# A decoder layer on one core: the first input projection issued between the first transposes, its weights moved up, the low-rank weights moved back

## The chip, the cores and the metric

The kernel runs on one core of a Trainium2 chip. The metric is the device time of one execution in microseconds (us); lower is better. Five engines work side by side, each from its own queue and in the order of that queue: TensorE (PE; its weight loads are PEld), VectorE (DVE), ScalarE (ACT), GpSimd (POOL) and SyncE (SP), which here issues the DMAs.

## The reference

One layer of a decoder trunk on 1024 tokens of width 1024, in float32. The part at the beginning of the kernel is the norm of the tokens and the mixer's input projection:

```python
h = _rms_norm(x, norm_pre_mix[i])
...
p = h @ w_in.astype(h.dtype)
u = p[..., :GLU_COLS]
q = p[..., GLU_COLS:]
q = q + (_token_shift(q) - q) * mu.astype(h.dtype)
...
r, k, v = q[..., :o1], q[..., o1:o2], q[..., o2:o3]
wd, ad, gd = q[..., o3:o4], q[..., o4:o5], q[..., o5:o6]
wf = (decay_w0 + jnp.tanh(wd) @ decay_up).astype(jnp.float32)
...
a = jax.nn.sigmoid(iclr_a0 + ad @ iclr_up)
g = jax.nn.sigmoid(gd) @ gate_up
```

Behind it come a recurrence over the tokens (eight heads of 64), a causal convolution of width 31 on a gated part of the projection, the output projection, a second norm, and a feed-forward part with a convolution of width 3 and 2816 channels. Both parts add their normed results to x.

## The kernel before

The tokens are worked on in two halves of 512 (`h` is 0 or 1). Channels lie on the 128 partitions, so the rows of x (128 tokens each) are normed and then transposed on TensorE. Every float32 operand of a projection is split in two, a rounded `hi` (or `wh` for weights) and the rest `lo` (`wl`), and three matmuls are added: wh x hi, wh x lo, wl x hi.

**The beginning.** `setup` loads an identity matrix (`const`, first 128 columns), all parameters (`params`) and the other constants; `setup_mixer` allocates, loads the low-rank weights (`lora`, and two pieces through the ring `wr` into `lw`, split by an ACT cast, line 232, and a POOL subtraction, line 234), and scales parameters on DVE (lines 238 to 247). `mixer` loads four rows of x (lines 281 to 285, eight DMAs of 256 KB), and then for each pair of rows, which is 256 tokens, runs `norm_rows` and `channels`. `norm_rows` takes the mean square of the first row of a pair on ACT (line 302) and that of the second on DVE (`bn_stats`, line 295), raises to the power -0.5 on POOL (line 153) and scales each row, its first half on ACT (line 305) and its second on DVE (line 306). `channels` transposes (line 146) into four PSUM banks of two channel blocks each (tags `pe` and `pb`), and evicts each block with the norm's weight: `hi` on ACT (line 271), `lo` on DVE (line 273). Both need `params`.

**The projections.** `project` multiplies one block of 128 output columns (64 for `w`, the low-rank inputs of decay and rate). Its weights come in two pieces of 256 KB, one for channel blocks 0 to 3 and one for 4 to 7. `weight` loads a piece into `wr` (a ring of three buffers), casts it to `wh` on ACT and subtracts on POOL to `wl` (line 158; `wh` and `wl` have two buffers each, so a cast waits until PE has done with the piece two before). For the first token half, `wl` is also stored to DRAM (`lows`, line 179), and the second token half loads it from there. The very first projection (`halves`, block 0 of `k0`) is done in two groups of 24 matmuls over 256 tokens each; all others are 24 matmuls over 512. The order of the first ones is k0 (two blocks), w, k1 (two), r0 (two), r1 (two). Then the elementwise work of the first quarter of the tokens begins.

**What sets the order.** The kernel is written for a planner, which orders each engine's instructions in a modelled timeline: of what is ready, it takes that with the lowest number first. A number is normally the place in the program; a `stream` gives its block numbers that begin elsewhere (first -1000, rwkv 1000, norm 200000, conv 300000, proj 400000), and `high_priority`, which `weight` and `shift` use, sets it to 0. On the chip, each engine then follows its planned order. `issue_after` puts instructions of an engine behind a named one of the same engine.

Of the kernel before, what the change touches and what calls it, by code (L numbers as in the profile page):

```python
# [21 lines left out]
P = 128  # L22
# [72 lines left out]
class Trunk:  # L95
# [87 lines left out]
    def setup(self):  # L183
# [13 lines left out]
        nc.sync.dma_start(self.params, a["params"])  # L197
        nc.sync.dma_start(self.const[:, P:], a["consts"][:, P:])
# [10 lines left out]
    def setup_mixer(self, ctx):  # L209
# [13 lines left out]
        self.Y = self.psum.tile([P, 512], F32, name="Y")  # L223


        self.lora = cp.tile([G_LORA, D_RWKV], F32, name="lora")
        nc.sync.dma_start(self.lora, a["lora"][:G_LORA, 2])
        self.lw = cp.tile([96, 2, D_RWKV], F32R, name="lw")
# [6 lines left out]
        self.lx = cp.tile([96, 2, QUARTER], F32R, name="lx")  # L235
        n = POFF["k_k"]
        self.omu = cp.tile([P, n], F32, name="omu")
        nc.vector.tensor_scalar(self.omu, self.params[:, :n], -1.0, 1.0, ALU.mult, ALU.add)

        self.hw0 = cp.tile([P, 8], F32, name="hw0")  # L240
        nc.vector.tensor_scalar(self.hw0, self.params[:, POFF["w0"]:POFF["w0"] + 8], 0.5, None, ALU.mult)
        self.ka = cp.tile([P, 8], F32, name="ka")
# [5 lines left out]
        self.carry = cp.tile([P, n], F32, name="carry")  # L248
        self.ccarry = cp.tile([P, 4, CONV_W - 1], F32, name="ccarry")
# [31 lines left out]
    def load_rows(self, h, rows):  # L281
        for t, row in enumerate(rows):
            rs = slice(h * HALF + t * P, h * HALF + (t + 1) * P)
            for j in range(2):
                self.nc.sync.dma_start(row[j], self.a["x"][rs, j * 512:(j + 1) * 512])

    def norm_rows(self, rows):

        nc = self.nc
        for t, row in enumerate(rows):  # L290
            ss = self.small.tile([P, 4], F32, tag="ss", name=self.nm("ss"))
            if t % 2:
                bs = self.small.tile([P, 4, 6], F32, tag="gn", bufs=3, name=self.nm("bs"))[:, 0:2]
                for j in range(2):
                    nc.vector.bn_stats(bs[:, j], row[j])
# [10 lines left out]
            nc.vector.tensor_scalar(row[1], row[1], ss[:, 3:4], None, ALU.mult)  # L306


    def project(self, src, m, hs, halves=False, kept=None):


        ps = self.bank()
        low = lambda j: kept and (kept[0], self.lows[kept[1], j])
        if halves:
            ws = [self.weight(src[j], [P, 4, m], kept=low(j)) for j in range(2)]
            for ts in (slice(0, 256), slice(256, 512)):
                for k in range(KT):
                    (wh, wl), (hi, lo) = ws[k // 4], hs[k]
                    self.mm(ps[:m, ts], wh[:, k % 4], hi[:, ts], start=k == 0, stop=False)
                    self.mm(ps[:m, ts], wh[:, k % 4], lo[:, ts], start=False, stop=False)  # L320
                    self.mm(ps[:m, ts], wl[:, k % 4], hi[:, ts], start=False, stop=k == KT - 1)
            return ps
# [759 lines left out]
    def mixer(self, sts):  # L1082
# [85 lines left out]
        with self.stream("norm"):  # L1168
            two = [self.tl("l8", [P, 2, D]) for _ in range(2)]
            rows = [cut(two[t // 2][:, t % 2]) for t in range(4)]  # L1170
            with self.stream("first"):
                self.load_rows(0, rows)
# [7 lines left out]
        project(0, hs, "k0 w k1 r0 r1")  # L1180
# [129 lines left out]
```

## Time and profile before

| what | us |
|---|---|
| median of three runs | 1310.73 |
| lowest and highest | 1307.76, 1311.3 |
| the profiled execution | 1310.48 |
| its span in the profile | 1308.7 |

The profile shows one execution. Its times count from the start of the span, and the 1.8 us between the execution's time and its span lie around it. A group "x4" in a timeline row is four instructions in a row; the two numbers at its beginning are its start and its length, and the brackets at its end say how long the engine had been idle and for what it had waited. Matmuls overlap one another, so the distance of their starts says more of their rate than their durations.

### The profile page before, as it was taken

To read this page: it belongs to the slowest core of one execution; us is meant where nothing else is said; L and a number is where in the kernel's file an instruction comes from. 1 tells how busy PE (TensorE), PEld (TensorE's weight loads), DVE (VectorE), ACT (ScalarE), POOL (GpSimd) and SP (SyncE) were. 2 spreads that over 40 slices of the span, in tenths; PEclk is the share of its full clock that TensorE was granted. 3 is DMA by queue.
4 is the path that set the end of the run, shared out by engine and by line. 5 is a ranking of instruction groups with operands and counts; after the bars stand their busy time and mean duration, and the time that the engine had idled before them with its cause. 6 is when DMAs were issued, how large, how long until landed. Compare 5 with 4: busy or idle time off the path is not lost.

```text
span 1308.7 us, 22940 instructions
## 1 busy us (share of the span) xinstructions
PE 1260.4 (96%) x8580; PEld 1018.6 (78%) x8580; DVE 864.0 (66%) x1520; ACT 678.4 (52%) x1354; POOL 462.6 (35%) x412
## 2 busy tenths in 40 slices
PE   5999989999999989999999999999999999999996
PEld 4767767777779867878799788888888888888884
DVE  5276997996789989995521364355455438479567
ACT  6563663656855765657642464443433445444451
POOL 4343320111123322444462466676766540000001
PEclk9999989999999989999999999999999999999998
DMA  6554332243333351222354765666564433335326
GB/s 236 160 146 125 115 112 90 83 145 113 115 110 106 119 181 43 73 66 78 100 161 126 265 211 167 194 183 195 173 207 137 120 92 113 94 110 164 105 65 209
DMA packets 97167, 176.77 MB, mean 135 GB/s; under 512 B 10560, under 2 KB 17088, under 8 KB 97056
## 3 DMA queue, kind: packets, MB, share of 16 engines
q1 hardware_dynamic: 97056, 175.31, 43.5%
q8 instruction: 67, 1.10, 0.4%
q14 instruction: 44, 0.36, 0.1%
HBM read 139.62 MB, written 35.65 MB: 134 GB/s over the span
## 4 chain that ended last, share of the span: by engine, by line
PE 77%; DVE 14%; ACT 4%; DMA 2%; issue 2%; POOL 1%; SPq 0%; POOLq 0%; ACTq 0%; DVEq 0%
PE pb L131 63%; PE pe L131 5%; DVE pc L410 4%; PE pn L131 3%; PE xs L131 3%; DVE dw L587 1%; PE pe L146 1%; DMA x<-x1d 1%; DVE pt L479 1%; DVE nrow L971 1%; DMA pt<-mixd 1%; DVE kk L480 1%; POOL wl L158 1%; PE pc L146 0%; DVE m L158 0%
## 5 line engine op out<-in xcount | busy, mean ns | idle before, releaser
L131 PE MATMUL pb<-f,wh 128*128 128x512 f32 x1408 | 444.5, 396 | 3.6 <-ACT pb L782 1.8
L158 POOL TENSOR_TENSOR wl<-wr,wh 128x512 fp32r<-128x512 f32 (+1 forms) x240 | 316.3, 1319 | 360.9 <-ACT wh L158 332.4
L158 ACT CAST wh<-wr 128x512 fp32r<-128x512 f32 (+1 forms) x279 | 171.5, 615 | 296.0 <-PE pb L131 142.3
L131 PEld LDWEIGHTS pb<-f,wh 128*128 128x128 f32 x1408 | 265.1, 189 | 63.9 <-ACT pb L782 2.0
L131 PE MATMUL pb<-f,wl 128*128 128x512 f32 x704 | 280.6, 399 | 1.7 <-POOL wl L158 1.5
L131 PE MATMUL pb<-h,wh 128*128 128x512 f32 (+3 forms) x720 | 230.0, 399 | 1.9 <-ACT wh L158 1.0
L888 DVE SCALAR_TENSOR_TENSOR acc<-pb,params,acc 128x511 f32<-128x511 f32 (+1 forms) x128 | 95.4, 745 | 184.8 <-ACT acc L883 124.0
L410 DVE SCALAR_TENSOR_TENSOR pc<-c,params,pc 128x512 f32<-128x512 f32 x232 | 174.1, 751 | 8.3 <-ACT pc L407 4.4
L131 PEld LDWEIGHTS pb<-f,wl 128*128 128x128 f32 x704 | 133.1, 189 | 34.6 <-POOL wl L158 3.9
L131 PEld LDWEIGHTS pb<-h,wh 128*128 128x128 f32 (+2 forms) x720 | 132.0, 189 | 34.4 <-ACT wh L158 2.7
L131 PE MATMUL pb<-h,wl 128*128 128x512 f32 (+3 forms) x360 | 146.3, 406 | 2.7 <-POOL wl L158 2.5
L153 POOL TENSOR_TENSOR ss<-var,mhalf 128x1 f32<-128x1 f32 x16 | 11.0, 693 | 229.7 <-DVE ss L952 203.3
L131 PE MATMUL pb<-w,a 128*128 128x512 f32 x366 | 89.8, 393 | 0.0
L131 PEld LDWEIGHTS pb<-h,wl 128*128 128x128 f32 (+2 forms) x360 | 67.8, 188 | 21.8 <-POOL wl L158 5.1
L131 PE MATMUL pb<-wh,a 128*128 128x512 f32 x240 | 81.5, 396 | 0.0
L131 PEld LDWEIGHTS pb<-w,a 128*128 128x128 f32 x366 | 68.7, 188 | 16.1
L928 POOL TENSOR_TENSOR b<-b,b 128x512 f32<-128x512 f32 x44 | 57.0, 1295 | 0.9
L888 DVE SCALAR_TENSOR_TENSOR pt<-pb,params,pt 128x511 f32<-128x511 f32 (+1 forms) x48 | 35.7, 744 | 31.5 <-ACT ecarry L885 31.0
L131 PEld LDWEIGHTS pb<-wh,a 128*128 128x128 f32 x240 | 45.1, 188 | 10.6
L700 POOL TENSOR_TENSOR XG<-r,GE 64x256 f32<-64x256 f32 x30 | 20.8, 696 | 85.5 <-DVE r L719 80.8
L883 ACT ACTIVATE acc<-pb,params 128x512 f32<-128x512 f32 x64 | 49.5, 773 | 1.8 <-PE pb L131 1.8
L131 PE MATMUL pb<-wl,a 128*128 128x512 f32 x120 | 47.7, 397 | 0.0
(301 smaller groups left out, 2038.8 us busy)
## 6 DMA issues: line engine op xcount, KB each, us to landing
wr<-ffn_up SPq DMA_DIRECT2D x176, 256.0 KB, 2.7
wr<-w_in SPq DMA_DIRECT2D x80, 256.0 KB, 2.9
b<-ffn_down SPq DMA_DIRECT2D x44, 256.0 KB, 3.9
sums<-b SPq DMA_DIRECT2D x44, 256.0 KB, 2.4
wr<-sums SPq DMA_DIRECT2D x44, 256.0 KB, 2.7
lows<-wl SPq DMA_DIRECT2D x40, 256.0 KB, 3.2
wl<-lows SPq DMA_DIRECT2D x40, 256.0 KB, 2.6
wr<-ffn_down SPq DMA_DIRECT2D x33, 256.0 KB, 2.7
```

Source lines behind the costliest of these rows:

```text
L131: return self.nc.tensor.matmul(out, lhsT, rhs, start=start, stop=stop, skip_group_check=skip)
L146: self.nc.tensor.transpose(out, in_, self.con("ident")[:n, :n])
L158: return self.nc.scalar.copy(hi, src), eng.tensor_tensor(lo, src, hi.bitcast(F32), ALU.subtract)
L410: nc.vector.scalar_tensor_tensor(out, c[:, j:j + HALF], w(j), acc, ALU.mult, ALU.add)
L479: nc.vector.tensor_tensor_scan(sg[:, l], self.con("scan"), sg[:, l], 0.0, ALU.mult, ALU.add)
L480: nc.vector.scalar_tensor_tensor(kk[:, l], k[:, l], self.par("k_k", 2 * pp + l), kk[:, l], ALU.mult, ALU.mult)
L587: nc.vector.tensor_tensor(dv[:, j + 1:, :j], dv[:, j + 1:, :j], tv, ALU.add)
L700: nc.gpsimd.tensor_tensor(x[64:128], R[64:128, gs], w.GE[64:128, c, gs].unsqueeze(2).broadcast_to([64, 4, CH]), ALU.mult)
L883: nc.scalar.activation(acc, ps, AF.Identity, scale=w(2), bias=self.par("fb", ch))
L888: nc.vector.scalar_tensor_tensor(acc[:, o:], ps[:, :HALF - o], w(j), acc[:, o:], ALU.mult, ALU.add)
L928: sub = lambda o, x, y, op=ALU.subtract: nc.gpsimd.tensor_tensor(o, x, y, op)
L971: nc.vector.tensor_tensor(out, a, b, op)
```

## The change

The loads of `params` and of the other constants are taken from `setup`. In `mixer`, inside the stream "first", the loads of the first two rows are followed by the two pieces of the first projection's weights (`self.first`, by `weight`, with its cast, its subtraction and its store), the load of `params`, the loads of the other two rows, and the other constants. `project` takes those weights for its first block, and its result is accumulated in the bank `pc` instead of `pb`. The low-rank loads, casts and subtractions become `low_rank`, called behind the projections k0 and w; the parameter scalings become `scales`, called ahead of k0. In `norm_rows`, the second `bn_stats` of an odd row is put behind the scaling of the row before it on DVE.

```diff
@@ -194,8 +194,6 @@
         self.const = cp.tile([P, NCONST], F32, name="const")
         with self.stream("first"):
             nc.sync.dma_start(self.const[:, :P], a["consts"][:, :P])
-        nc.sync.dma_start(self.params, a["params"])
-        nc.sync.dma_start(self.const[:, P:], a["consts"][:, P:])
         self.mhalf = cp.tile([P, 8], F32, name="mhalf")
         nc.gpsimd.memset(self.mhalf, -0.5)
         self.mixd = self.dp.tile([SEQ, D], F32, name="mixd")
@@ -221,32 +219,40 @@
         self.dw = cp.tile([P, 16 + 1024], F32, name="dw")
         nc.gpsimd.memset(self.dw[0:64, 528:1040], 0.0)
         self.Y = self.psum.tile([P, 512], F32, name="Y")
-
-
         self.lora = cp.tile([G_LORA, D_RWKV], F32, name="lora")
+        self.lw = cp.tile([96, 2, D_RWKV], F32R, name="lw")
+        self.lx = cp.tile([96, 2, QUARTER], F32R, name="lx")
+        n = POFF["k_k"]
+        self.omu = cp.tile([P, n], F32, name="omu")
+        self.hw0 = cp.tile([P, 8], F32, name="hw0")
+        self.ka = cp.tile([P, 8], F32, name="ka")
+        self.carry = cp.tile([P, n], F32, name="carry")
+        self.ccarry = cp.tile([P, 4, CONV_W - 1], F32, name="ccarry")
+
+    def low_rank(self):
+
+
+        nc, a = self.nc, self.a
         nc.sync.dma_start(self.lora, a["lora"][:G_LORA, 2])
-        self.lw = cp.tile([96, 2, D_RWKV], F32R, name="lw")
         for e in range(2):
             raw = self.wp.tile([P, D_RWKV], F32, tag="wr", bufs=3, name=self.nm("wr"))
             nc.sync.dma_start(raw, a["lora"][:, e])
             nc.scalar.copy(self.lw[:, e], raw[0:96])
             low = self.lw[64:96, e]
             nc.gpsimd.tensor_tensor(low, raw[64:96], low.bitcast(F32), ALU.subtract)
-        self.lx = cp.tile([96, 2, QUARTER], F32R, name="lx")
+
+    def scales(self):
+
+        nc = self.nc
         n = POFF["k_k"]
-        self.omu = cp.tile([P, n], F32, name="omu")
         nc.vector.tensor_scalar(self.omu, self.params[:, :n], -1.0, 1.0, ALU.mult, ALU.add)
 
-        self.hw0 = cp.tile([P, 8], F32, name="hw0")
         nc.vector.tensor_scalar(self.hw0, self.params[:, POFF["w0"]:POFF["w0"] + 8], 0.5, None, ALU.mult)
-        self.ka = cp.tile([P, 8], F32, name="ka")
         ka = self.params[:, POFF["k_a"]:POFF["k_a"] + 4]
         nc.vector.tensor_scalar(self.ka[:, 0:4], ka, 0.5, None, ALU.mult)
         nc.vector.tensor_scalar(self.ka[:, 4:8], ka, -0.5, 1.0, ALU.mult, ALU.add)
         cw = self.params[:, POFF["cw"]:POFF["cw"] + 4 * CONV_W]
         nc.vector.tensor_scalar(cw, cw, 0.5, None, ALU.mult)
-        self.carry = cp.tile([P, n], F32, name="carry")
-        self.ccarry = cp.tile([P, 4, CONV_W - 1], F32, name="ccarry")
 
 
     def channels(self, rows, gname, hs, toks, tags=("pn",), diags=None):
@@ -278,8 +284,8 @@
     def pairs(self, what, pool=None):
         return [self.pair(what, pool or self.hp) for _ in range(KT)]
 
-    def load_rows(self, h, rows):
-        for t, row in enumerate(rows):
+    def load_rows(self, h, rows, t0=0):
+        for t, row in enumerate(rows, t0):
             rs = slice(h * HALF + t * P, h * HALF + (t + 1) * P)
             for j in range(2):
                 self.nc.sync.dma_start(row[j], self.a["x"][rs, j * 512:(j + 1) * 512])
@@ -287,12 +293,14 @@
     def norm_rows(self, rows):
 
         nc = self.nc
+        scaled = None
         for t, row in enumerate(rows):
             ss = self.small.tile([P, 4], F32, tag="ss", name=self.nm("ss"))
             if t % 2:
                 bs = self.small.tile([P, 4, 6], F32, tag="gn", bufs=3, name=self.nm("bs"))[:, 0:2]
-                for j in range(2):
-                    nc.vector.bn_stats(bs[:, j], row[j])
+                nc.vector.bn_stats(bs[:, 0], row[0])
+                with self.tc.issue_after(scaled.ins):
+                    nc.vector.bn_stats(bs[:, 1], row[1])
                 nc.vector.bn_aggr(ss[:, 0:2], bs)
 
                 nc.vector.scalar_tensor_tensor(ss[:, 2:3], ss[:, 0:1], ss[:, 0:1], ss[:, 1:2], ALU.mult, ALU.add)
@@ -303,16 +311,16 @@
                 nc.vector.tensor_tensor(ss[:, 2:3], ss[:, 0:1], ss[:, 1:2], ALU.add)
             self.rstd(ss[:, 3:4], ss[:, 2:3], 1.0 if t % 2 else 1.0 / D, RMS_EPS)
             nc.scalar.activation(row[0], row[0], AF.Copy, scale=ss[:, 3:4])
-            nc.vector.tensor_scalar(row[1], row[1], ss[:, 3:4], None, ALU.mult)
+            scaled = nc.vector.tensor_scalar(row[1], row[1], ss[:, 3:4], None, ALU.mult)
 
 
     def project(self, src, m, hs, halves=False, kept=None):
 
 
-        ps = self.bank()
+        ps = self.bank("pc" if halves else "pb")
         low = lambda j: kept and (kept[0], self.lows[kept[1], j])
         if halves:
-            ws = [self.weight(src[j], [P, 4, m], kept=low(j)) for j in range(2)]
+            ws = self.first
             for ts in (slice(0, 256), slice(256, 512)):
                 for k in range(KT):
                     (wh, wl), (hi, lo) = ws[k // 4], hs[k]
@@ -1169,7 +1177,12 @@
             two = [self.tl("l8", [P, 2, D]) for _ in range(2)]
             rows = [cut(two[t // 2][:, t % 2]) for t in range(4)]
             with self.stream("first"):
-                self.load_rows(0, rows)
+                self.load_rows(0, rows[:2])
+                i = 4
+                self.first = [self.weight(self.a["w_in"][i][j], [P, 4, P], kept=(0, self.lows[i, j])) for j in range(2)]
+                nc.sync.dma_start(self.params, self.a["params"])
+                self.load_rows(0, rows[2:], 2)
+                nc.sync.dma_start(self.const[:, P:], self.a["consts"][:, P:])
             hs = self.pairs("h")
             for b in range(2):
                 two = rows[2 * b:2 * b + 2]
@@ -1177,7 +1190,10 @@
                 self.channels(two, "pre_mix", hs, slice(b * QUARTER, (b + 1) * QUARTER), ("pe", "pb", "pb"))
         self.R = self.tl("r", [P, NH, CH])
         nc.vector.memset(self.R[64:128], 0.0)
-        project(0, hs, "k0 w k1 r0 r1")
+        self.scales()
+        project(0, hs, "k0 w")
+        self.low_rank()
+        project(0, hs, "k1 r0 r1")
         with self.stream("norm"):
             two = self.tl("mixr", [P, 2, D])
             rows = [cut(two[:, t]) for t in range(2)]
```

## The prediction

> **What bounds the kernel now.** I read the page first: how full each engine is.
>
> ```profile
> span 1308.7 us, 22940 instructions
> PE 1260.4 (96%) x8580; PEld 1018.6 (78%) x8580; DVE 864.0 (66%) x1520; ACT 678.4 (52%) x1354; POOL 462.6 (35%) x412
> ```
>
> TensorE is busy for 1260.4 of 1308.7 us, so only 48.3 us are idle in the whole run. The change reorders the first 60 us; next comes the table of engines by stretch (columns: stretch, length, busy us of PE, PEld, DVE, ACT, POOL, clock, DMA).
>
> ```profile
> 0.00:10.00 10.00, 1.06 (x4) 0.58 (x4) 2.74 (x9) 4.34 (x9) 1.38 (x8) 1.00 0.71 234
> 10.00:20.00 10.00, 7.05 (x29) 5.36 (x28) 7.77 (x27) 8.72 (x22) 5.44 (x6) 1.00 1.06 370
> 20.00:30.00 10.00, 8.75 (x56) 7.66 (x55) 7.44 (x24) 8.33 (x20) 5.33 (x7) 1.00 0.36 120
> 30.00:40.00 10.00, 10.00 (x45) 6.85 (x44) 1.63 (x4) 3.14 (x7) 3.82 (x4) 1.00 0.50 147
> ...
> 50.00:60.00 10.00, 10.00 (x44) 7.97 (x43) 2.23 (x5) 5.04 (x8) 4.98 (x4) 1.00 0.65 202
> ```
>
> From 30 to 60 us PE is full (first and last of three rows); before that it idles 8.94 + 2.95 + 1.25 = 13.1 us. That is all the head could give if nothing had to be waited for. From 10 to 20 us ScalarE is the fullest engine (8.72) and the DMA engines are saturated (1.06). Where PE stands is seen in its timeline.
>
> ```profile
> 18.10 1.09 PE L146 MATMUL pb<-const,l 128*128 128x128 f32 x4 [0.63 <-DVE h L273]
> 20.91 0.76 PE L131 MATMUL pb<-h,wh 128*128 128x256 f32 x2 [0.48 <-DVE h L273]
> 21.47 0.41 PE L131 MATMUL pb<-h,wl 128*128 128x256 f32 x1
> 22.11 0.41 PE L131 MATMUL pb<-h,wl 128*128 128x256 f32 x1
> 23.30 0.28 PE L131 MATMUL pb<-h,wl 128*128 128x256 f32 x1
> 24.44 0.39 PE L131 MATMUL pb<-h,wl 128*128 128x256 f32 x1 [0.63 <-POOL wl L158]
> 25.26 0.28 PE L131 MATMUL pb<-h,wl 128*128 128x256 f32 x1
> 25.62 0.28 PE L131 MATMUL pb<-h,wl 128*128 128x256 f32 x1
> 28.62 0.63 PE L131 MATMUL pb<-h,wh 128*128 128x512 f32 x2
> 29.39 0.50 PE L131 MATMUL pb<-h,wl 128*128 128x512 f32 x1
> 40.50 1.02 PE L131 MATMUL pb<-h,wh 128*128 128x512 f32 x2
> 41.36 0.40 PE L131 MATMUL pb<-h,wl 128*128 128x512 f32 x1
> ```
>
> The first projection starts at 20.91, after all 32 transposes, and the second takes over at 28.62: 7.7 us for 48 matmuls. Three of them take 22.11 - 21.47 = 0.64 us at first (0.213 each) and 25.62 - 25.26 = 0.36 us later (0.12 each), so PE changes to a faster clock near 23.2 us, though the column of the granted clock says 1.00 throughout. The head's transposes run at the slow rate too, (1.09 - 0.42)/3, about 0.22 us apart (0.42 is the slow one's duration in the head).
>
> **The change part by part.**
>
> *Loads.* SyncE issues in order; these are its issue rows, and below them the sizes and times from issue to landing.
>
> ```profile
> 5.43 0.71 SPq L198 DMA_DIRECT2D const<-consts  x1
> 6.18 0.66 SPq L227 DMA_DIRECT2D lora<-lora  x1
> 9.78 0.33 SPq L166 DMA_DIRECT2D wr<-w_in  x1
> ```
>
> ```profile
> wr<-lora SPq DMA_DIRECT2D x2, 256.0 KB, 5.5
> wr<-w_in SPq DMA_DIRECT2D x1, 256.0 KB, 5.5
> const<-consts SPq DMA_DIRECT2D x1, 224.5 KB, 7.3
> lora<-lora SPq DMA_DIRECT2D x1, 192.0 KB, 7.2
> ```
>
> The last of x, parameters and constants lands at 5.43 + 7.3 = 12.7 us; the low-rank weights follow, and the first projection weight lands at 9.78 + 5.5 = 15.3. In the code the new weight loads stand behind the first 256 tokens, but `weight` sets the planner's number to 0 while the loads around it are in the stream "first", at -1000 and up. A planner that takes the lowest number first would issue parameters, the other 256 tokens and the constants before them. I forecast with that order. Then the weights take the place of `lora` and its successors: the 256 KB from 13.4 (where `lora`'s 192 KB landed, 6.18 + 7.2), the second 256 KB (15.3 - 13.4)/3 = 0.63 later, at 14.0. The tokens of rows 2 and 3 only get the parameters' 185 KB ahead of them, 0.5 us at the 370 GB/s of the table. The three low-rank loads (704 KB) leave the stretch where DMA is saturated.
>
> *Casts and subtractions.* ACT, DVE and POOL in the timeline:
>
> ```profile
> 14.56 0.62 ACT L232 CAST lw<-wr 96x512 fp32r<-96x512 f32 x1
> ...
> 16.93 0.62 ACT L158 CAST wh<-wr 128x512 fp32r<-128x512 f32 x1
> 20.46 0.84 ACT L271 ACTIVATE h<-pe,params 128x256 fp32r<-128x256 f32 x2
> ```
>
> ```profile
> 8.49 0.69 DVE L295 BATCH_NORM_STATS2 bs<-l 128x6 f32<-128x512 f32 x1 [1.88 <-DMA l<-x]
> 9.10 0.47 DVE L306 TENSOR_SCALAR l<-l,ss 128x512 f32<-128x512 f32 x1
> 12.48 0.21 DVE L247 TENSOR_SCALAR params<-params 128x124 f32<-128x124 f32 x1
> 21.46 0.87 DVE L273 SCALAR_TENSOR_TENSOR h<-pe,params,h 128x256 fp32r<-128x256 f32 x2
> ```
>
> ```profile
> 13.60 0.55 POOL L153 TENSOR_TENSOR ss<-var,mhalf 128x1 f32<-128x1 f32 x1 [0.69 <-DVE var L152]
> 15.31 2.50 POOL L234 TENSOR_TENSOR lw<-wr,lw 32x512 fp32r<-32x512 f32 x2 [1.16 <-ACT lw L232]
> 17.89 1.27 POOL L158 TENSOR_TENSOR wl<-wr,wh 128x512 fp32r<-128x512 f32 x1
> 28.01 1.32 POOL L158 TENSOR_TENSOR wl<-wr,wh 128x512 fp32r<-128x512 f32 x1 [0.36 <-ACT wh L158]
> 35.55 0.74 POOL L158 TENSOR_TENSOR wl<-wr,wh 128x256 fp32r<-128x256 f32 x1 [0.66 <-ACT row L338]
> ```
>
> ACT loses two low-rank casts (2 x 0.62 us) among its evictions and gains the second weight's (0.62): 0.6 us relief, against 0.5 us later tokens; I take zero, bounds 0.6 either way, as PE is the later one below. POOL loses 2.50 us there and gains 1.3. First `wl`: 13.4 + 0.62 cast + 0.1 + 1.27 = 15.4 us; the second 1.27 later, 16.7. POOL's last power (13.60, now about 14.1) may stand one subtraction later, 1.3 us; that delays the last row's scaling, whose transposes PE has other work beside.
>
> *The first projection between the transposes.* PE has about 14 transposes of the second 256 tokens left at 15.4, plus 24 matmuls of the first half, then the 24 of the second: 62 units. The trace has no such mixture, so I bound when the clock becomes fast: 2.3 us after start (counted from the matmuls at 20.91 to 23.2) or 5.1 us (from the nearly gapless transposes at 18.10). With slow units of 0.22 and fast ones of 0.12 the end is 15.4 + 2.3 + 51.5 x 0.12 = 23.9, or 15.4 + 5.1 + 39 x 0.12 = 25.2. I take the middle, 24.6. Its lower bound is the eviction chain: DVE ends at 21.46 + 0.87 = 22.3, plus three matmuls, 22.7. So the second projection takes over 28.62 - 24.6 = **4.0 us** earlier (5.9 at the bound). The Trainium skill, "TensorE: Matmul & The Clock Gate", Part 1, says the clock doubles after some 3.4 us of sustained work; by that the end would be 24.4, an estimate inside my two bounds.
>
> The added wait is PE's on `wl`: behind it in PE's queue stand the second tokens' transposes, and ACT and DVE wait for those. Their evictions end at 22.3 now, so up to some 2 us are covered by PE's own end at 24.6.
>
> *What is late next.* The third weight's cast waits for the first `wh` to be released, 12 matmuls before the projection's end; today that is 28.62 - 12 x 0.12 = 27.2, and `wl` comes at 28.01 + 1.32 = 29.3, just ahead of 29.39. Both shift together: nothing lost.
>
> *Order on DVE.* `bn_stats` of a row's second half now waits for the scaling of the row before. Today the scaling (9.10) stands behind a `bn_stats` that waited for its tokens until 8.49; it gets earlier by over a microsecond. For the second pair the later `bn_stats` waits for POOL's power instead; behind it on DVE are the evictions. I cost both at nothing (bounds 0.5 either way), under PE's bound. The five parameter scalings (0.17 to 0.21 us each) stay under 1 us wherever they stand.
>
> *Low-rank work behind two projections.* Two loads into the shared `wr` ring of three, `lora`, two casts of 0.62 and two subtractions of 1.25. ACT is busy 3.14 and POOL 3.82 of 10 us there (30 to 40), so the work itself is hidden. The ring is what can cost: k1's first weight, today fetched right after the fourth `wr` use, now waits for the slot of the sixth, released by POOL at 35.55 + 0.74 = 36.3. A weight takes this to land (page):
>
> ```profile
> wr<-w_in SPq DMA_DIRECT2D x80, 256.0 KB, 2.9
> ```
>
> 36.3 + 0.1 + 2.9 + 0.62 + 1.29 = 41.2 against PE's first need at 41.36 (all times of before): hidden with 0.1 us to spare. If the landing takes a microsecond more, that microsecond shows. I take 0, bounds 0 to 1.0. If the cover (PE's 5.5 us on `w`) were absent, it would cost all 4.9 us of that sum.
>
> *After that.* PE is full to 60 us, so the shift stays whole that far, and the later work depends on these projections; I take it that all of it moves with them. Sum: -4.0, bounds -5.9 - 0.6 and -(28.62 - 25.2) + 1.0 + 1.3, so -6.5 to -1.1. The profiled execution took 1310.48 us (span 1308.7 and 1.8 around it), the median is 1310.73: **1306.7 us**, which is 0.31% less. A measurement of this kernel can tell about 0.3% (3.9 us) from no change, so the forecast lies on that border.
>
> **The rivals.**
>
> 1. *The clock stays slow in the mixture.* For: head transposes from 8 to 20 us never became fast. Then 38 units from 15.4 take 38 x 0.22 = 8.4, to 23.8; another 2.3 us slow (10 matmuls), 14 fast: 27.8. Gain 0.8, 1309.9 us. Against: the faster rate came within 2.3 us of the first matmul, and the mixture has 24. The Trainium skill, same page, Part 4, says that transposes do not count as busy work for the gate in the same way; the slow transposes here agree.
>
> 2. *It does what it says*: weights really land behind 256 tokens. Both have landed at 8.5 + 512 KB / 370 GB/s = 9.9 (8.49 is where the second row's second half had landed), `wl` follows by 11.8, and the first half is done while the other tokens come 1.4 us later still. Then the eviction bound decides, 22.3 + about 1 = 23.3: gain 5.3, 1305.4 us. Against: the planner's numbers.
>
> 3. *Slower: the planner's new order costs VectorE time later.* The kernel is ordered by a modelled timeline, and any shift can reorder every engine. The place that could pay is the second half's transposes:
>
> ```profile
> L410 DVE SCALAR_TENSOR_TENSOR pc<-c,params,pc 128x512 f32<-128x512 f32 x49 | 36.8, 750 | 1.1 <-ACT pc L407 0.3
> ```
>
> These are convolution steps of 0.75 us between 130 and 200 us, where PE waits for the DVE evictions interleaved with them. From six such steps ahead of the evictions on (6 x 0.75 = 4.5), the gain is gone; with ten it is 3.5 us slower, 1314.2. Against: evictions carry a lower number than the convolution.
>
> 4. *The ring makes k1 late*: ACT and POOL take both low-rank pieces first, 2 x 0.62 + 2.50 less 0.1 of slack, 3.6 us: 1310.3. Against: the weights' own casts and subtractions carry the number 0, lower than the low-rank ones.
>
> **How the numbers follow.** Forecast 0.50, rivals 0.14, 0.09, 0.17 and 0.10. The forecast's own range, 1304.2 to 1309.6, has a little over half of its chance below 1306.8 (0.3% faster): 0.30, the rest within 0.3%. Rival 2 adds 0.08 to faster; a reordering as in 3 can also gain, and I put 0.08 of the forecast's chance there instead of at its upper end. Rivals 1 and 4 are within 0.3% (0.22 of their 0.24, 0.02 slower). Rival 3 is slower. Faster 0.46, same 0.35, slower 0.19. The range 1301.5 to 1312.5 takes in all bounds, rivals 1, 2 and 4, and the milder part of 3.
>
> **What would show it.** Matmuls of line 131 between transposes of line 146 from about 15.4 us; the second projection (first 512-wide matmuls) near 24.6 instead of 28.62; two weight issues near 6 us on SyncE, behind the constants or, in rival 2, ahead of the third row; 0.36 us per three matmuls before 21 us or not (rival 1); no PE wait on `wl` at the projection behind `w` (rival 4); the same 4 us still there at 57, 130 and 200 us (rival 3). Wrong would be a head that gains 4 us and a span that does not, or PE standing at `wl` with transposes behind it.

## The result: slower, with the head as forecast

| | before | after |
|---|---|---|
| median, us | 1310.81 | 1318.03 |
| lowest to highest (4 runs each) | 1307.76 to 1311.3 | 1316.85 to 1319.29 |
| profiled execution, us | 1310.48 | 1317.42 |
| its span, us | 1308.7 | 1315.6 |
| ratio of the times | | 1.006, 95% interval 1.0037 to 1.0083 |

The changed kernel is 0.6% slower. 1318.03 us lies above the forecast (1306.7) and outside its range (1301.5 to 1312.5). The two profiled executions differ by 6.9 us, so the profile shows the loss. First the page of the changed kernel, span and engines:

```profile
span 1315.6 us, 22926 instructions
PE 1258.5 (96%) x8580; PEld 1017.3 (77%) x8580; DVE 870.9 (66%) x1520; ACT 678.4 (52%) x1353; POOL 458.7 (35%) x412
```

PE's busy time is 1.9 us less than before although the span is 6.9 longer: the loss is idle time of PE. Where it is, the table by stretch tells (stretch, length, busy us of PE, PEld, DVE, ACT, POOL, clock, DMA share, GB/s). The head of the changed kernel:

```profile
0.00:10.00 10.00, 1.25 (x4) 0.58 (x4) 3.49 (x14) 4.50 (x9) 1.38 (x8) 1.00 0.71 236
10.00:20.00 10.00, 8.03 (x38) 7.34 (x39) 7.61 (x18) 7.14 (x17) 4.11 (x5) 1.00 1.06 374
20.00:30.00 10.00, 9.51 (x61) 8.34 (x60) 8.99 (x21) 8.10 (x22) 3.65 (x4) 1.00 0.38 130
```

PE is busy for 18.79 of the first 30 us, against 1.06 + 7.05 + 8.75 = 16.86 before. The head works better, not worse. PE's timeline there, in the changed kernel:

```profile
15.37 0.58 PE L131 MATMUL pc<-h,wh 128*128 128x256 f32 x1 [0.49 <-DVE h L279]
15.75 0.41 PE L131 MATMUL pc<-h,wl 128*128 128x256 f32 x1
16.18 0.41 PE L146 MATMUL pe<-const,l 128*128 128x128 f32 x1
19.54 0.28 PE L131 MATMUL pc<-h,wl 128*128 128x256 f32 x1
20.94 0.60 PE L146 MATMUL pe<-const,l 128*128 128x128 f32 x4
24.50 0.62 PE L131 MATMUL pb<-h,wh 128*128 128x512 f32 x2
36.72 1.03 PE L131 MATMUL pb<-h,wh 128*128 128x512 f32 x2
37.63 0.50 PE L131 MATMUL pb<-h,wl 128*128 128x512 f32 x1
```

The first projection (`pc`) runs between the transposes (line 146), the second takes over at 24.50 instead of 28.62, and k1's first block starts at 36.72 instead of 40.50. That is 4.1 and 3.8 us earlier. Then the same table for three late stretches, first of before, then of after:

```profile
240.00:330.00 90.00, 89.84 (x1051) 71.31 (x1050) 76.81 (x127) 57.28 (x116) 12.12 (x18) 1.00 0.39 121
330.00:640.00 310.00, 296.64 (x2938) 242.88 (x2937) 263.70 (x479) 198.70 (x429) 108.71 (x97) 0.98 0.32 98
640.00:1340.00 700.00, 653.97 (x3010) 537.25 (x3009) 351.18 (x577) 287.69 (x547) 266.04 (x211) 0.99 0.47 147
```

```profile
240.00:330.00 90.00, 85.98 (x1010) 68.31 (x1009) 70.47 (x118) 54.80 (x109) 9.62 (x15) 0.96 0.35 110
330.00:640.00 310.00, 292.05 (x2919) 238.76 (x2918) 261.33 (x477) 191.73 (x419) 103.70 (x95) 0.99 0.32 97
640.00:1340.00 700.00, 659.64 (x3041) 541.75 (x3039) 356.79 (x583) 294.83 (x561) 269.11 (x214) 0.99 0.48 148
```

PE idles 4.02 us between 240 and 330 us (0.16 before) and 17.95 between 330 and 640 (13.36 before). At 640 us it has 659.64 us of work left against 653.97: a lead of about 4 us has become a lag of about 6. A finer account asks at what time PE has done the same amount of matmul work in both traces (columns counted over all matmuls; worked out from the matmul records, so an ordinary table). Negative is ahead of before:

| at (us of before) | 30 | 60 | 130 | 180 | 240 | 260 | 330 | 440 | 640 | 1300 |
|---|---|---|---|---|---|---|---|---|---|---|
| after | -3.8 | -3.6 | -3.6 | -3.9 | -3.7 | +2.2 | +4.1 | +7.7 | +7.4 | +6.9 |

The lead of the head stays whole for 200 us. Then 5.9 us go at one place, between 240 and 260, and about 5 more up to 440. Behind 640 nothing changes. The one place, in the changed kernel: PE's waits from 200 to 270 us (us in total, times, longest), its timeline, and DVE's:

```profile
PE xs L146 <- DVE r L727: 2.9, 2, 2.1
```

```profile
254.29 0.45 PE L146 MATMUL xs<-const,v 128*64 128x128 f32 x2 [2.06 <-DVE r L727]
255.54 0.64 PE L146 MATMUL xs<-const,v 128*64 128x128 f32 x2 [0.80 <-DVE r L727]
256.82 1.05 PE L131 MATMUL pb<-h,wh 128*128 128x512 f32 x2
```

```profile
246.71 7.07 DVE L418 SCALAR_TENSOR_TENSOR pc<-c,params,pc 128x512 f32<-128x512 f32 x9
253.81 0.43 DVE L727 TENSOR_TENSOR r<-xs,XG 64x256 f32<-64x256 f32 x1
255.05 0.43 DVE L727 TENSOR_TENSOR r<-xs,XG 64x256 f32<-64x256 f32 x1
```

Nine convolution steps in a row (line 418, 7.07 us) stand ahead of two sums of the recurrence (line 727), for which PE waits with four transposes. In the window from 200 to 270 us of before, PE waits for nothing. Its DVE timeline has the same pieces:

```profile
250.44 7.07 DVE L410 SCALAR_TENSOR_TENSOR pc<-c,params,pc 128x512 f32<-128x512 f32 x9
257.67 0.74 DVE L344 SCALAR_TENSOR_TENSOR row<-pb,params,row 128x511 f32<-128x511 f32 x1
259.90 0.43 DVE L719 TENSOR_TENSOR r<-xs,XG 64x256 f32<-64x256 f32 x1
```

There the sum also comes late (259.90), but on PE the transposes that need it stand behind more projection matmuls: the first two run at 262.33, with no wait. So neither engine does other work than before. The two queues are interleaved in another way.

The waits are about half of the loss here. The clock column of 240 to 330 us has 0.96 where before has 1.00, which is (1 - 0.96) x 90 = 3.6 us of PE's full rate; two matmuls of 512 columns take 1.05 us at 256.82, against 0.62 at 24.50. With the 3.9 us more of idle time that makes 7.5 of the 7.8 us that the lag table loses from 240 to 330. That the waits bring the slow stretch about was not tried by itself.

### The profile page after: what moved, and what is told of

Its sections match the earlier page's. It is cut to its first block, busy times and chain, and to the rows that moved or that the text cites. A ratio compares the mean times of both kernels' runs of the same rounds, so it can differ in the third digit from the quotient of the medians.

```text
span 1315.6 us, 22926 instructions
## 1 busy us (share of the span) xinstructions
PE 1258.5 (96%) x8580; PEld 1017.3 (77%) x8580; DVE 870.9 (66%) x1520; ACT 678.4 (52%) x1353; POOL 458.7 (35%) x412
## 4 chain that ended last, share of the span: by engine, by line
PE 74%; DVE 16%; DMA 4%; ACT 2%; issue 2%; POOL 1%; SPq 1%; POOLq 0%; ACTq 0%; DVEq 0%
PE pb L131 61%; DVE pc L418 5%; PE pe L131 4%; PE pn L131 3%; PE xs L131 3%; POOL wl L158 1%; DMA pt<-mixd 1%; DVE dw L595 1%; DVE sub L593 1%; DMA x<-x1d 1%; PE pe L146 1%; DVE nrow L979 1%; DMA wr<-ffn_up 1%; DMA mixd<-t 1%; PE pc L146 1%
## 5 line engine op out<-in xcount | busy, mean ns | idle before, releaser
L131 PE MATMUL pb<-f,wh 128*128 128x512 f32 x1408 | 442.2, 395 | 3.1 <-ACT pb L790 1.8
L131 PEld LDWEIGHTS pb<-f,wh 128*128 128x128 f32 x1408 | 263.5, 188 | 61.9 <-ACT pb L790 2.0
L131 PE MATMUL pb<-f,wl 128*128 128x512 f32 x704 | 280.1, 398 | 2.8 <-POOL wl L158 2.7
L131 PE MATMUL pb<-h,wh 128*128 128x512 f32 (+2 forms) x688 | 224.6, 405 | 2.0 <-ACT wh L158 1.0
L131 PEld LDWEIGHTS pb<-f,wl 128*128 128x128 f32 x704 | 132.5, 188 | 36.7 <-POOL wl L158 6.2
L131 PEld LDWEIGHTS pb<-h,wh 128*128 128x128 f32 (+2 forms) x688 | 127.2, 188 | 34.9 <-ACT wh L158 4.0
L131 PE MATMUL pb<-h,wl 128*128 128x512 f32 (+2 forms) x344 | 141.1, 410 | 2.1 <-POOL wl L158 2.0
L131 PE MATMUL pb<-w,a 128*128 128x512 f32 x366 | 89.8, 393 | 0.0
L131 PE MATMUL pb<-wh,a 128*128 128x512 f32 x240 | 81.5, 396 | 0.0
L131 PEld LDWEIGHTS pb<-w,a 128*128 128x128 f32 x366 | 68.8, 188 | 16.1
L131 PEld LDWEIGHTS pb<-h,wl 128*128 128x128 f32 (+2 forms) x344 | 64.7, 188 | 20.4 <-POOL wl L158 4.4
L131 PEld LDWEIGHTS pb<-wh,a 128*128 128x128 f32 x240 | 45.2, 188 | 10.6
L131 PE MATMUL pb<-wl,a 128*128 128x512 f32 x120 | 47.7, 397 | 0.0
L158 DVE TENSOR_TENSOR a<-act,a 128x512 fp32r<-128x512 f32 x50 | 33.5, 695 | 18.3 <-ACT a L158 18.3
```

Source lines behind the costliest of these rows:

```text
L131: return self.nc.tensor.matmul(out, lhsT, rhs, start=start, stop=stop, skip_group_check=skip)
L158: return self.nc.scalar.copy(hi, src), eng.tensor_tensor(lo, src, hi.bitcast(F32), ALU.subtract)
```

## The experiments

Two theories stood against each other. **Order**: nothing in the head costs anything; the planner lays out the later work in another order, because its modelled timeline begins otherwise, and that order is worse. **Resources**: what the change moves (low-rank work behind two projections, the weights' ring, the loads, the edge on `bn_stats`) delays something later. To tell them apart, the order of each engine from k1's first projection on was taken from one planned kernel and imposed on another; the lists hold the same 10,573 instructions from there on. The order is imposed by edges that only the planner sees, which add no wait on the chip (abridged):

```python
def pin(tc, trunk):
    ...
        for a, b in zip(mine, mine[1:]):
            tc.add_manual_dep(b, a.name, DependencyInfo(NoSync, DATA), reason="planned order")
```

`mine` is one engine's list. "Pinned" below means this list, of the kernel before unless another is named; in kernels with the change, or the edge on `bn_stats`, pinned to before's order, that edge stands for the first 512 tokens alone, since for the others the list decides. "Free" means ordered by the planner. The list stands in a kernel's code, so the line numbers of a pinned kernel are higher: L202 and L161 are the matmul of L131, and L217 and L176 the transpose of L146. All results (the ratio is to the kernel before, run beside it; the last column is the start of the second projection in the profile):

| run | median, us | ratio, 95% interval | second projection |
|---|---|---|---|
| e1_pin | 1304.33 | 0.9951, 0.9932 to 0.997 | 23.27 |
| e2_cross | 1322.07 | 1.0084, 1.0068 to 1.0101 | 28.32 |
| e3_nobn | 1313.36 | 1.0022, 1.0011 to 1.0034 | 23.50 |
| e4_lowrank_front | 1325.17 | 1.0106, 1.0083 to 1.0128 | 24.82 |
| e5_spot | 1317.97 | 1.0061, 1.004 to 1.0082 | 23.16 |
| e6_pin_lowrank_only | 1309.82 | 0.9996, 0.9982 to 1.001 | 29.16 |
| e7_pin_lowrank_front | 1309.36 | 0.9986, 0.997 to 1.0002 | 25.23 |
| e8_pin_weights_early | 1306.96 | 0.998, 0.9967 to 0.9994 | 26.52 |
| e9_half_pin | 1310.6 | 0.9993, 0.9979 to 1.0007 | 23.19 |
| e10_null_free | 1325.92 | 1.01, 1.0073 to 1.0128 | 29.12 |
| e11_null_pin | 1311.03 | 1.0, 0.9988 to 1.0012 | 29.59 |
| e12_pin_nobn | 1305.68 | 0.9954, 0.9935 to 0.9972 | 25.09 |

And how far PE was ahead (-) or behind (+) of before, counted as above:

| run | 60 | 180 | 240 | 260 | 330 | 440 | 640 | 1300 |
|---|---|---|---|---|---|---|---|---|
| e1_pin | -4.6 | -4.7 | -6.8 | -6.8 | -6.7 | -6.8 | -8.1 | -7.9 |
| e2_cross | -0.1 | -0.4 | +0.6 | +6.6 | +8.5 | +12.1 | +12.0 | +12.5 |
| e5_spot | -4.7 | -5.0 | -4.7 | -4.6 | +3.1 | +6.7 | +5.7 | +5.9 |
| e9_half_pin | -4.6 | -4.8 | -6.7 | -6.7 | -6.7 | -4.9 | -1.2 | -1.1 |
| e10_null_free | +0.5 | +0.5 | +2.9 | +6.6 | +11.9 | +8.9 | +15.8 | +15.5 |
| e11_null_pin | +1.5 | +1.5 | +0.5 | +0.5 | +0.5 | +0.5 | -0.7 | -0.3 |

### The head of one kernel, the order of the other

e1_pin is the changed kernel with before's order from k1 on (the list and `pin` itself are left out of this cut):

```diff
-        Trunk(ctx, tc, a).run()
+        trunk = Trunk(ctx, tc, a)
+        trunk.run()
+        pin(tc, trunk)
```

> The changed kernel, but from the first k1 projection on every engine gets its instructions in the order that the planner had made for the kernel before (the second bn_stats is put behind the scaling only for the first 512 tokens, since the old order has it otherwise for the others). Theory 1, order: the head gives 3.7 us and all of the loss comes from the planner's other order of the work between 250 and 640 us, so the median is 1307.1 us (1306 to 1308), and PE's progress leads the kernel before by 3.6 to 3.8 us from 30 us to the end. Theory 2, resources: the moved low-rank work, the weight ring or the loads collide with work behind and cost 11 us in any order; then about 1318.

e2_cross is the opposite: the kernel before, with the same lines and the list of the changed kernel.

> The kernel before with its own head, but from the first k1 projection on with the order that the planner made for the changed kernel. Theory 1, order: it keeps the loss of the mixer (7.4 + 3.7 = 11.1 us) and lacks the gain of the head, so 1310.8 + 11.1 = 1321.9 us (1319 to 1323). Theory 2, resources: 1310 to 1312, as nothing of the change's parts is in it.

e1_pin took 1304.33 us (10 runs, 1300.1 to 1309.85): 0.49% faster than before, and 13.7 less than the changed kernel's 1318.03. That is below the 1306 to 1308 expected, and its lead grows behind 180 us instead of staying as it was (last section). e2_cross took 1322.07, as expected: 0.84% slower than before, with a head that is not changed at all. The same table by stretch of e1_pin:

```profile
240.00:330.00 90.00, 89.83 (x922) 71.52 (x922) 76.80 (x131) 60.60 (x124) 12.07 (x17) 1.00 0.40 121
640.00:1340.00 700.00, 646.13 (x2975) 530.49 (x2973) 349.04 (x573) 284.67 (x541) 261.75 (x208) 0.99 0.47 146
```

PE idles 0.17 us from 240 to 330, as before the change, and at 640 us it has 7.8 us less left than before. In e2_cross the stretch looks like that of the changed kernel:

```profile
240.00:330.00 90.00, 87.08 (x996) 67.98 (x994) 72.30 (x120) 52.94 (x105) 11.21 (x18) 0.96 0.37 115
```

So the loss goes with the order and not with the head, and e1_pin beats both kernels.

### An edit that should cost nothing, free and pinned

The smallest part of the change, the edge on `bn_stats`, was put into the kernel before, once free (e10_null_free) and once pinned (e11_null_pin):

```diff
-                for j in range(2):
-                    nc.vector.bn_stats(bs[:, j], row[j])
+                nc.vector.bn_stats(bs[:, 0], row[0])
+                with self.tc.issue_after(scaled.ins):
+                    nc.vector.bn_stats(bs[:, 1], row[1])
```

> The kernel before with only the order edge of the second bn_stats, planner free: an edit of the head that is worth 0.5 us at most there. Theory 1, order: the planner reorders the mixer here too, and the end may lie anywhere from 1302 to 1325 us, more than 2 us off the kernel before, with PE's shift made between 180 and 640 us and not in the head. If the planner's order is stable against such edits, the median is 1309 to 1312.

> The kernel before with the order edge of the second bn_stats for the first 512 tokens, in the planned order of the kernel before from k1 on. Theory 1: the edge alone is worth 0.5 us at most, so the median is 1309.5 to 1311.5.

Free it costs 14.5 us (1325.92 against 1311.41 beside it, and above the range expected); pinned it costs nothing (1311.03, ratio 1.0). In both the second projection starts about where it did before (29.12 and 29.59 against 28.62). What PE has left at 640 us, e10_null_free first:

```profile
640.00:1340.00 700.00, 666.56 (x3056) 546.71 (x3056) 358.76 (x586) 294.36 (x561) 272.93 (x216) 0.99 0.48 149
```

```profile
640.00:1340.00 700.00, 653.66 (x3008) 536.57 (x3006) 351.24 (x576) 287.52 (x547) 266.20 (x211) 0.99 0.47 147
```

12.9 us of work lie between them, from an edit in the head. One thing differs beside the order of the rest: in the free kernel the edge stands in the norm of the other 512 tokens too. With the list, those `bn_stats` stand where they stood before. Up to 180 us the free kernel is only 0.5 us behind, so the edge costs next to nothing where it stands; this pair alone does not show that it costs nothing further on, but e2_cross loses in the same way with no such edge in it.

### Other parts of the change, free

e3_nobn is the changed kernel without the edge on `bn_stats`:

```diff
-                with self.tc.issue_after(scaled.ins):
-                    nc.vector.bn_stats(bs[:, 1], row[1])
+                nc.vector.bn_stats(bs[:, 1], row[1])
```

> The changed kernel without the order edge of the second bn_stats; the planner is free. Theory 1, order: PE's lead is 3 to 4.5 us up to 240 us, as with the edge, and the end is anything from 1304 to 1320, by what order the planner falls on. Theory 2 with the edge as the cause: 1307. Rival on the head: the edge is worth something in the head; then the first 512-wide matmul starts later than 24.50 us, by up to 0.5.

e4_lowrank_front is the changed kernel with the low-rank work ahead of the projections again:

```diff
-        project(0, hs, "k0 w")
         self.low_rank()
-        project(0, hs, "k1 r0 r1")
+        project(0, hs, "k0 w k1 r0 r1")
```

> The changed kernel with the low-rank loads, casts and subtractions called ahead of k0 instead of behind w; the planner is free. Theory 1, order: the first 512-wide matmul still starts within 1 us of 24.50, PE's lead at 240 us is 2.5 to 4 us, and the end is anything from 1304 to 1320. Theory 2 with the low-rank work behind w as the cause: 1307.

1313.36 and 1325.17 us, the second above its range. Both heads keep most of the lead (4.1 and 2.5 us at 130 us, counted as in the tables), and both lose it at other places than the changed kernel: e3_nobn between 300 and 440 us, e4_lowrank_front mostly between 380 and 510. Four free kernels (with the changed one and e10_null_free) thus span 12.6 us (1313.36 to 1325.92), while their heads differ by 4.6 us at 60 us (from 4.1 ahead in e3_nobn to 0.5 behind in e10_null_free). Before, whose head gains nothing, is faster than all four. Neither run says anything of the part it was made for, because the order changed with it; that was then asked with the order held.

### The same parts, pinned

e12_pin_nobn is e1_pin without the edge; e6_pin_lowrank_only is the kernel before with nothing but the low-rank work moved behind two projections; e7_pin_lowrank_front is e1_pin with that work in front again. The call of e6 (its function and the list are left out of the cut; e7 calls it ahead of k0):

```diff
-        project(0, hs, "k0 w k1 r0 r1")
+        project(0, hs, "k0 w")
+        self.low_rank()
+        project(0, hs, "k1 r0 r1")
```

> The pinned kernel of the first experiment without the order edge of the second bn_stats. Its planner-free form had the second projection at 23.50 us. Theory: the edge is worth nothing, the median is within 1.5 us of the pinned kernel with it, 1303 to 1306; if the edge is worth its wait on DVE, it is 1306 to 1308.

> The kernel before with only the low-rank loads, casts and subtractions moved behind k0 and w, in the planned order of the kernel before from k1 on. By the prediction's terms ScalarE gets rid of two casts (1.2 us) among its evictions and the ring costs 0 to 1.0 us at k1: the first projection starts at 20.0 to 20.9 us and the median is 1310 to 1311.5. If the ring is what hurts, PE waits at the first k1 projection for wl by over 1 us and the median is above 1312.

> The changed kernel with the low-rank work ahead of k0, in the planned order of the kernel before from k1 on. If the first projection between the transposes is the part that gains, PE's lead at 60 us is 2.4 to 4 us and the median 1305 to 1308; if the moved low-rank work is what made the gain of the pinned kernel, it is 1309 to 1311.

The edge is worth nothing that can be told (0.9954 without, 0.9951 with), though the two profiled heads lead by 2.6 and 4.6 us at 60 us. The low-rank work moved alone gives nothing either (0.9996): the first projection starts at 21.65 in its profile, against 20.91 before and 20.0 to 20.9 expected, since it waits for the tokens and not for the weights. Yet with the weights moved up it matters: put in front again, it gives 0.9986 instead of e1_pin's 0.9951. PE's timeline of e7_pin_lowrank_front shows where:

```profile
25.23 0.73 PE L202 MATMUL pb<-h,wh 128*128 128x512 f32 x2 [0.32 <-ACT wh L229]
26.64 0.50 PE L202 MATMUL pb<-h,wl 128*128 128x512 f32 x1 [0.68 <-POOL wl L229]
```

The second projection starts 2.0 us later than in e1_pin. The two waits, for a cast and a subtraction, are part of it; the first projection also begins 0.8 us later (15.32 against 14.56). The lead at 60 us is 2.1 us against 4.6. The medians lie further apart than that, about 4.6 us by the ratios, and the mean granted clock of all runs differs too (0.9857 here, 0.9886 in e1_pin), so the price of the low-rank work in front is known only roughly.

### The weights really behind 256 tokens

In the changed kernel the weights' loads are issued behind all of x, parameters and constants (SyncE, changed kernel):

```profile
3.07 0.43 SPq L1183 DMA_DIRECT2D params<-params  x1
3.54 1.86 SPq L291 DMA_DIRECT2D l<-x  x4
5.45 0.58 SPq L1185 DMA_DIRECT2D const<-consts  x1
6.08 2.12 SPq L166 DMA_DIRECT2D wr<-w_in  x3
```

e8_pin_weights_early lets the first two weights keep the number of the stream "first", which puts their loads where the code has them, pinned from k1 on:

```diff
-        with self.tc.high_priority():
+        with self.tc.high_priority() if hasattr(self, "first") else ExitStack():
```

> The pinned kernel of the first experiment, but with the first projection's weights issued right behind the first 256 tokens, ahead of the parameters and the other tokens (rival 2 of the prediction). By the sum there the second projection starts at 23.3 us against 24.5 in the changed kernel, and the median is 1303 to 1306. If the later tokens decide, it starts at 25 us or later and the median is 1305 to 1308.

1306.96 us, and the second projection at 26.52: 3.3 us later than in e1_pin. The numbers are those of the second reading, but its reason is not what the trace shows. The last of the other rows is scaled earlier than in e1_pin (15.99 against 16.74). What comes later is the second row of the first 256 tokens, scaled at 12.50 against 11.17. On VectorE the parameter scalings stand ahead of its mean square; they wait until 9.55 for `params` (8.30 in e1_pin), whose load is now behind the weights, and one of them takes 1.24 us while POOL subtracts. So the first projection begins at 15.79 instead of 14.56. In this execution PE also stays at the slow rate until about 21.7 us, in e1_pin until about 15 (last section). That the planner's order is the better one is likely, no more: the intervals of 0.998 and 0.9951 overlap a little.

### One wait removed, and a half list

e5_spot is the changed kernel pinned to its own order, but with the two sums of line 727 taken ahead of the last four and three of the nine convolution steps on DVE (a sketch of DVE's queue; in the code only the list differs):

```text
-  conv conv conv conv conv conv conv conv conv sum conv sum conv
+  conv conv conv conv conv sum conv sum conv conv conv conv conv
```

> The changed kernel with its own planned order from k1 on, except for two VectorE instructions: the two sums of the recurrence (line 727 of the changed kernel) that stood behind nine convolution steps at 253.8 us now stand behind five and six of them. If this place costs what the trace says (PE idle 2.9 us between 252 and 256, then some 11 matmuls at the slow clock, 2.3 us more), PE's idle time there falls below 1 us and the median to 1313 to 1315.5 us. Rival, the wait only moves on to the next step of the recurrence: PE's lag behind the kernel before is again 2 us at 300 us and the median stays at 1317 to 1319.

This missed, and the rival's range held: 1317.97, no better than 1318.03. The wait at 254 us is gone, and two others stand in its place (PE's waits from 200 to 330 us; then the table by stretch):

```profile
PE pb L202 <- ACT wh L245: 2.1, 1, 2.1
PE pb L202 <- DVE row L423: 1.3, 1, 1.3
```

```profile
260.00:264.00 4.00, 2.78 (x12) 2.17 (x12) 3.89 (x7) 0.00 (x0) 0.00 (x0) 1.00 0.25 66
264.00:268.00 4.00, 1.30 (x7) 0.59 (x6) 3.08 (x7) 2.99 (x5) 0.00 (x0) 0.92 0.10 33
```

The eviction that PE waits for, and ACT's work ahead of the cast `wh`, are in the timelines of DVE (e5_spot, then the changed kernel) and ACT (e5_spot):

```profile
260.33 0.74 DVE L423 SCALAR_TENSOR_TENSOR row<-pb,params,row 128x511 f32<-128x511 f32 x1
```

```profile
261.32 0.75 DVE L352 SCALAR_TENSOR_TENSOR row<-pb,params,row 128x511 f32<-128x511 f32 x1
```

```profile
264.93 0.78 ACT L486 ACTIVATE pc<-c,params 128x512 f32<-128x512 f32 x1 [7.87 <-DVE co L489]
265.65 0.60 ACT L245 CAST wh<-wr 128x512 fp32r<-128x512 f32 x1
```

DVE had no gap up to there and is busy for 3.89 of 4 us. The eviction comes 1.0 us earlier, which is the lead of e5_spot's head, and not 2.9: up to it DVE has the same work in either order. The cast comes late because ACT has stood for 7.87 us at an instruction that waits for a convolution step. With this order DVE is the bound of the stretch, and moving an instruction within its queue moves the wait. Of the 1.7 us by which the table has e5_spot ahead at 640 us (+5.7 against +7.4), 1.1 are its lead at 60 us (-4.7 against -3.6). The slow clock moves with the waits: 240 to 260 us has none in e5_spot, and 264 to 268 has 0.92.

e9_half_pin is e1_pin with the list cut off near 330 us; the planner goes on from there.

> The changed kernel with the order of the kernel before only from k1 to about 330 us; behind that the planner is free. If the loss is made in that stretch (the +5.6 us at 255 us, and what follows from a planner that goes on from another state), PE's lead of 3.5 to 7 us at 260 us is still there at 600 us and the median is 1303 to 1307. If the mixer behind 330 us loses by itself, the lead falls by 3 to 5 us between 330 and 640 us, and the median is 1308 to 1312.

1310.6 us, the second of the two readings. To 330 us it holds the lead of 6.7; then it loses 5.5 of them to waits that e1_pin has not, or has shorter (e9_half_pin, then e1_pin, PE's waits from 330 to 640 us):

```profile
PE pb L161 <- POOL wl L188: 3.7, 4, 1.4
PE pb L161 <- DVE f L309: 3.2, 3, 2.1
PE pe L176 <- DVE mixr L792: 2.2, 1, 2.2
```

```profile
PE pb L202 <- POOL wl L229: 2.1, 3, 0.9
PE pb L202 <- DVE f L350: 1.8, 3, 0.9
PE pe L217 <- DVE mixr L833: 1.0, 1, 1.0
```

So there is no single bad place. Each stretch that the planner lays out anew can lose some us, and mending one wait by hand moves it to the next.

## Why the prediction was wrong, step by step

- **Loads: right.** The planner issued parameters, the other 256 tokens and the constants ahead of the weights. The casts of the weights began at 12.76, somewhat before the 13.4 worked out.
- **The first projection: right in its time, not in what it waits for, and in part by luck.** PE was to wait for the weights' `wl`, ready at 15.4. POOL subtracted both pieces from 13.44 to 15.94, and PE's wait ahead of its first `wl` matmul (15.75) was for `lo` of the tokens: 0.49 us at 15.37, on DVE. POOL's last power came at 15.89, behind both subtractions; the prediction allowed for one. The second projection took over at 24.50 (forecast 24.6, 4.0 us earlier; it was 4.1). The three rows from 19.54 to 24.50 show the fast rate before 20 us, between transposes, so rival 1 is out. The four transposes of 20.94 take 0.60 us together, against 1.09 for four at 18.10 of before. But 24.6 was the middle of two bounds for the clock (23.9 and 25.2), and the same head took 23.27 and 23.16 in e1_pin and e5_spot, below both (last section).
- **What is late next: nearly right.** The third weight's `wl` was to stay just ahead of PE. PE waited 0.49 us for it at 25.61.
- **`bn_stats`: right by itself** (e12_pin_nobn against e1_pin), and wrong in what it does to the planner (e10_null_free). The parameter scalings were not tried alone; in e8_pin_weights_early they cost the head time.
- **Low-rank work and ring: right.** k1's first `wl` matmul ran at 37.63 with no wait, so rival 4 is out. Rival 2's order was tried in e8_pin_weights_early: its weights were there as early as the rival said (POOL subtracts from 8.80 to 11.30, 11.8 reckoned), but the second projection started at 26.52 and not 23.3, since the second row of the first tokens came later.
- **The step that failed is the last one: "I take it that all of it moves with them."** The later work did move with the projections for 200 us, and then not. A gain of 3.7 us at 240 us became a loss of 7.4 at 640. With before's order held, the change gives 0.49% (e1_pin; 0.3% to 0.68%), which is 6.4 us of 1311.19, interval 3.9 to 8.9: the 4.0 of the forecast lies in it, at its lower end. In e1_pin's profile 4.6 us are there at 60 us; the lead grows by 2.1 us between 180 and 240 us, with the clock, and by 1.3 between 440 and 640. How much of the 6.4 us is the clock's is not settled (last section).
- **Rival 3 had the mechanism, but not the place or the size.** It had convolution steps get ahead of what PE waits for, as at 246.71. It put them between 130 and 200 us, where the lead did not move, and limited them to ten steps at that place (1314.2 us). In fact it was 5.9 us in the recurrence near 250 us and 5 more from there to 440, by waits and by the slow clock beside them. It got 0.17; e3_nobn, e4_lowrank_front and e10_null_free show the same: every variant that was ordered freely ended above the kernel before run beside it, by 2.2 to 14.5 us, so more chance was due to it. The argument against it, that evictions carry a lower number than the convolution, did not protect the sums of the recurrence, ahead of which nine convolution steps were taken. A reading that was not tried: the planner takes the lowest number of what is ready in its modelled time, and those sums were not ready in it yet.

What stays open: why the modelled timeline misjudges these places was not tried. Nor which of the moved instructions matter; e5_spot and e9_half_pin only show that it isn't one.

## What to carry to other kernels

In a kernel whose whole order comes from a planner, an edit near the beginning is two edits: what it does, and the new order of all that follows, here up to 14.5 us of 1311, against 6.4 for the edit itself with the order held. Hold the order of the rest when the edit is judged, use an edit that should do nothing as control, and follow the lead of the bounding engine from stretch to stretch: a lead that is whole at 60 us says nothing of 640. If the edit is good and the new order is not, the old order can be kept (e1_pin).

## What the hardware showed beside this

TensorE's clock does not answer to the work alone. Over the same 20 us the table by stretch gives, for before, after and e1_pin:

```profile
184.00:204.00 20.00, 17.41 (x107) 13.13 (x107) 18.71 (x30) 9.79 (x19) 0.21 (x1) 0.66 0.20 63
```

```profile
184.00:204.00 20.00, 16.94 (x123) 12.92 (x122) 19.23 (x33) 7.32 (x14) 1.19 (x2) 0.74 0.10 27
```

```profile
184.00:204.00 20.00, 18.00 (x130) 14.07 (x132) 19.72 (x34) 7.22 (x13) 0.00 (x0) 0.83 0.17 53
```

A mean of 0.66, where the slow clock is 0.5 in the traces' records, is (1 - 0.66) x 2 x 20 = 13.6 us of slow clock; 0.74 gives 10.4 and 0.83 gives 6.8. These are four, three and two times 3.4 us. The Trainium skill, "TensorE: Matmul & The Clock Gate", Part 1, describes such a window of about 3.4 us that runs freely, and says that the same kernel therefore warms up after a different number of matmuls from run to run; the traces agree, by these multiples and by the three heads that follow.

The effect in the head: the changed kernel, e1_pin and e5_spot have the same code up to k1's first projection, and their second projection starts at 24.50, 23.27 and 23.16, with the fast rate from about 19 us in the first and 15 us in the two others. So some 1.3 us of a head go with the clock. So does the step of e1_pin's lead from 4.7 to 6.8 us near 190 us, where it has 6.8 us of slow clock less than before; e11_null_pin, with before's order and no gain in its head, shows 0.83 there as well, and makes a step of 1.0 us.

Whether that is chance alone, the runs do not settle. The mean granted clock of e1_pin's ten runs is 0.9886, that of the 21 runs of before beside it 0.9852 (the records begin with the first change to the fast rate, at 15 and 23 us in the two profiles, and what lies ahead counts as 1.00). Over mean spans of 1302.5 and 1309.1 us that is slow clock worth up to 14.8 and 19.4 us, so up to 4.6 of e1_pin's 6.4 us may lie there, and whether its head, its order or chance brings them was not tried. The spread of one kernel follows the clock too: e1_pin's run of 1309.85 us has 0.985 and that of 1300.66 has 0.993. That is a reason to compare medians of many runs, and the clock beside them.

Rival 1 rests on transposes not counting as work for the clock. Four transposes take 1.09 us in the head of before, but in e11_null_pin they became fast for about 3.4 us, before its first projection matmul at 21.44, and then slow again:

```profile
17.98 0.63 PE L217 MATMUL pb<-const,l 128*128 128x128 f32 x4 [0.58 <-DVE h L344]
19.09 1.09 PE L217 MATMUL pb<-const,l 128*128 128x128 f32 x4 [0.49 <-DVE h L344]
```

Here the measurement goes against the sentence that the rival cites: transposes alone can bring the fast clock.
